# One step of a hybrid streaming encoder layer: weight split ahead of operands in the output projection, chunk states in groups of two, cached gate sum behind them

## Chip, cores and metric

The kernel runs on one core of one Trainium2 chip. The metric is the device time of one execution in microseconds (us), taken as the median of three runs. Engines are named as the profile names them: PE is TensorE's matmul stream and PEld its weight loads, DVE is VectorE, ACT is ScalarE, POOL is GpSimd, SP is SyncE (which here only issues DMAs).

## The reference, cut to what matters

One layer over 16 learned meta tokens and 512 prompt frames, and over 32 frames of a running stream with a cache of 256 rows. All branch inputs and gates come from one input projection. The GLA branch (gated linear attention) carries a state from chunk to chunk; the FoX branch (softmax attention with forget gates) needs running sums of the gate logs, for the running stream over cache and new frames together.

```python
def _gla_chunks(q, k, v, log_a, s0):
    g = jnp.cumsum(log_a, axis=2)
    g_tot = g[:, :, -1]
    k_dec = k * jnp.exp(g_tot[:, :, None] - g)
    u = jnp.einsum('bnchk,bnchv->bnhkv', k_dec, v)
    def step(s, inp):
        a, uc = inp
        s = jnp.exp(a)[..., None] * s + uc
        return s, s
    s_last, s_all = lax.scan(step, s0, (jnp.moveaxis(g_tot, 1, 0), jnp.moveaxis(u, 1, 0)))
    ...
# running stream: gate sums over the cached rows and the new ones
c_all = jnp.cumsum(jnp.concatenate([cache_logf.astype(jnp.float32), logf], axis=-1), axis=-1)
...
def _merge_ffn(h, ya, yb, ga, gb, w_out, norm_ffn, w_up, w_down):
    m = jax.nn.sigmoid(ga) * ya + jax.nn.sigmoid(gb) * yb
    h = h + jnp.einsum('btd,de->bte', m, w_out)
    u = jnp.einsum('btd,df->btf', _rmsnorm(h, norm_ffn), w_up)
    return h + jnp.einsum('btf,fd->btd', jnp.square(jax.nn.relu(u)), w_down)
```

## The kernel before

**Numbers in two halves.** Almost every matrix product runs on numbers split into a high and a low half in the matmul's 32-bit format: `split_hi` (L121, ACT) copies a tile into the format, `split_lo` (L124, DVE) subtracts the copy from the tile. A product is then three matmuls (hi*hi, lo*hi, hi*lo) into one PSUM tile. Both helpers have one line each, so in the trace tiles tell instructions apart, not lines.

**Weight units.** The projections' weights are a list of units of 128 output columns. `use(key)` makes sure that the unit asked for and the one after it are prepared (`unit_prep`): SP loads the raw weights `wr` (three buffers), POOL scales those of the input projection by the norm's gain (L250), ACT makes `wh`, DVE makes `wl`; `wh` and `wl` have two buffers each. A product over a unit (`blocks_steps`) is 48 matmuls: 8 row blocks, three products, two spans of tokens (288 and 256 columns).

**The order of work.** Up to the output projection the instructions are put in order by the framework's scheduler, which follows the order of the code as a priority; generators (`gq_steps`, `token_major` and others) are advanced a few steps at a time (`go(steps, n)`, `drain(steps)`) so that matmuls of one job stand between those of another. From `tc.manual_schedule` (ahead of the feed-forward part) on, PE, ACT and DVE run exactly in code order. A wait holds up all that stands behind it on its engine.

**GLA chunk states (L654 to L674, called at L804 to L806).** For each of five token tiles t (two chunks each) `chunk_states(t)` issues 8 products `ps_u` of 64 x 128 (the profile counts 16 matmuls, since these are not split), into the PSUM tiles `psv` (one buffer) and `psa` (two buffers), and then, per chunk, two DVE instructions that make the chunk's state from the one before (`states`, L671). Ahead of each tile 16 matmuls of the projection `ps_gq` (unit gq 0) are let through (`GAP_STATE`). After the five tiles the rest of gq 0 and all of gq 1 follow, then the small transposition `ps_prm` (L392), `ps_oS`, and the projection `ps_fv`.

**Cached gate sum (L723 to L731).** Ahead of that, `lS` collects the cached gate logs (a DMA that POOL issues) and the new ones (a POOL copy), a DVE scan turns `lS` into `cS`, and POOL writes `cS` to DRAM (`cSd`), from where it is read in the attention part. `cP` and `cPd` are the same for the prompt.

**Output projection (L1294 to L1305).** Eight units `wo`, in the order 0, 4, 1, 5, 2, 6, 3, 7; n counts them in this order. For each: `use` (prepares unit n+1), some steps of `pair_prep(0)` (weights for the first feed-forward pair: after n = 1 the loads, at n = 2 sums on DVE, at n = 4 four splits, at n = 6 three), 48 matmuls `ps_wo`, two DVE additions that take them into `xres` (L1300), and `operands(d)`. The last makes the feed-forward's inputs out of the unit just ended: for the first unit of a pair (d < 4) two ACT scalings `ba`, `bb`, a DVE difference (L1254) and a split `hh`/`hl`; for the second one scaling `b`, two DVE sums (L1261, L1262), three splits with another sum (L1273) between. The feed-forward's first product, `ps_x`, needs `hh` and `hl` of all four first units.

Of the kernel before, what the change touches and what calls it, by code (L numbers as in the profile page):

```python
# [13 lines left out]
ALU = mybir.AluOpType  # L14

P = 128
D = 1024
KD = D // P
SEQ = 512
META = 16  # L20
SMP = 32
PAST = 256
H = 8
# [24 lines left out]
def tile_hybrid_step(  # L48
# [8 lines left out]
    TE, ACT, DVE, POOL, SP = nc.tensor, nc.scalar, nc.vector, nc.gpsimd, nc.sync  # L57
# [29 lines left out]
    def tmp(shape, name, dtype=F32):  # L87
        return blk(shape, dtype, name, "tmp")
# [117 lines left out]
    onerow = tmp([SEQ], "onerow")[0:H]  # L206
# [11 lines left out]
    def drain(steps):  # L218
        for _ in steps:
            pass  # L220

    def go(steps, n):
        for _ in range(n):
            next(steps, None)
# [34 lines left out]
    def use(key, ahead=1):  # L259
        idx = [u[0] for u in units].index(key)  # L260
        while nxt[0] < len(units) and nxt[0] <= idx + ahead:
            unit_prep(nxt[0])
            nxt[0] += 1
        return done.pop(key)
# [112 lines left out]
    WO_ORDER = (0, 4, 1, 5, 2, 6, 3, 7)  # L377
# [265 lines left out]
    def decays(t):  # L643
# [7 lines left out]
        kd = g1[t][:, 0:256]  # L651
        DVE.tensor_tensor(kd[:n], dec[:n], kd[:n], ALU.mult)

    def chunk_states(t):  # L654
        c0, n = TT[t]
        kd = g1[t][:, 0:256]
        puv = [f(f"ps_u{t}").rearrange("p (a v) -> p a v", v=P) for f in (psv, psa)]
        for c in range(2):
            r0, r1 = (((0, META), (32, 64)) if t == 0 else ((0, 64), (64, 128)))[c]
            for hh in range(GH):  # L660
                mm(puv[c][64 * (hh % 2): 64 * (hh % 2) + 64, hh // 2, :],
                   kd[r0:r1, 64 * hh: 64 * hh + 64], gv[t][r0:r1, P * hh: P * hh + P], True, True)
        for c in range(2):
            ch = 2 * t + c
            dst = sblk[ch // 6][:, ch % 6]
            if ch == 0:
                DVE.tensor_copy(dst, puv[0][:, 0:2, :])
            else:
                prev = st0 if ch == 1 else (states[0] if ch == 2 else states[ch - 1])
                for p in range(2):  # L670
                    DVE.scalar_tensor_tensor(dst[:, p, :], prev[:, p, :], eg[:, p, ch: ch + 1], puv[c][:, p, :],  # L671
                                             ALU.mult, ALU.add)
            states[ch] = dst
    for t in range(NTT):  # L674
        totals(t)
# [44 lines left out]
    cP = tmp([META + SEQ], "cP")[0:H]  # L720
    DVE.tensor_tensor_scan(cP[:, 0:META], onerow[:, 0:META], lfa[:, 0:META], 0.0, ALU.mult, ALU.add)
    DVE.tensor_tensor_scan(cP[:, META:], onerow, lfb, cP[:, META - 1: META], ALU.mult, ALU.add)
    lS = tmp([PAST + SMP], "lS")[0:H]  # L723
    POOL.dma_start(lS[:, 0:PAST], cache_logf[0, 0])
    POOL.tensor_copy(lS[:, PAST:], lfa[:, 32:64])
    cS = tmp([PAST + SMP], "cS")[0:H]
    DVE.tensor_tensor_scan(cS, onerow[:, 0: PAST + SMP], lS, 0.0, ALU.mult, ALU.add)
    cPd = tc.dram_tile([H, META + SEQ], F32, name="cPd")
    cSd = tc.dram_tile([H, PAST + SMP], F32, name="cSd")
    POOL.dma_start(cPd, cP)  # L730
    POOL.dma_start(cSd, cS)  # L731


    V = [None] * NTT
# [67 lines left out]
    go(gq[0], 1)  # L802
    fv_steps = fv_prepare()
    for t in range(NTT):  # L804
        go(gq[0], GAP_STATE)
        chunk_states(t)  # L806
    drain(gq[0])
    drain(gq[1])
    late_params()
    POOL.dma_start(o_sp[0, 0].rearrange("(p a) k v -> (a k) p v", a=2), states[9])  # L810
# [483 lines left out]
    for n, d in enumerate(WO_ORDER):  # L1294
        xr = xres[d]
        wh, wl = use(("wo", d))
        go(prep, {1: 1, 2: 2, 4: 4, 6: 3}.get(n, 0))

        def evac_o(ci, a, b, ps, xr=xr):
            DVE.tensor_tensor(xr[:, a:b], ps, xr[:, a:b], ALU.add)  # L1300

        blocks(f"wo{d}", range(KD), wh, wl, lambda k, a, b: mh[k][:, a:b], lambda k, a, b: ml[k][:, a:b],
               OC, evac_o, psany, both=n == 0)
        hs[d] = xr
        operands(d, n == KD - 1)  # L1305


    ffnL = ctx.enter_context(ExitStack())
# [346 lines left out]
```

## Time and profile before

| | before |
|---|---|
| three runs | 831.92, 834.13, 834.67 us |
| median | 834.13 us |
| the profiled execution | 829.3 us |
| its span, first to last instruction | 827.5 us |
| PE busy (share of the span) | 801.3 us (97%) |
| PEld busy | 770.3 us (93%) |
| DVE, ACT, POOL busy | 584.0 us (71%), 366.6 us (44%), 123.6 us (15%) |
| mean granted TensorE clock | 0.997 |

The profile is of one execution; its times are microseconds from the first instruction. A row of the timeline gives the start, the length, the engine, the line, the operation with output and inputs, the shape, the number of instructions that it merges, and in brackets how long the engine stood idle before it and what ended that. The ends of matmuls are modelled, so the start of the next row is the better mark of how long a stretch took. The chain of waits follows the work that ended last back through what released each step.

### The profile page before, as it was taken

What the parts mean: (1) busy time and instruction counts of PE and PEld (TensorE: products, weight loads), DVE (VectorE), ACT (ScalarE), POOL (GpSimd) and SP (SyncE); (2) the same over time, 40 slices, a digit from 0 to 9 for tenths busy, and PEclk for the clock granted to TensorE, in tenths of its full rate; (3) what the DMA queues carried; (4) which work ended last, traced back from release to release, by engine and by line L of the source; (5) the groups of instructions that cost most, each with busy time, mean ns of one, the idle gap of its engine ahead of it and who ended that gap; (6) DMA issues with size and microseconds to landing.
All of it is one profiled execution on the core that took longest, in us unless ns stands there. A gap on an engine that the chain in (4) does not pass through costs nothing.

```text
span 827.5 us, 15155 instructions
## 1 busy us (share of the span) xinstructions
PE 801.3 (97%) x6093; PEld 770.3 (93%) x6093; DVE 584.0 (71%) x1142; ACT 366.6 (44%) x722; POOL 123.6 (15%) x132
## 2 busy tenths in 40 slices
PE   8998999999999999999989999999999999999995
PEld 7877899898999989999989999999999999999995
DVE  5856348798768464466567987778777776799764
ACT  6760454555345532323355783343334433433433
POOL 4305112221121384014100000000000000000000
PEclk9999999999999999999999999999999999999998
DMA  8513214431531123233522143323333332331402
GB/s 248 154 46 104 51 44 103 124 78 51 128 90 51 50 74 108 77 90 91 152 66 58 47 121 108 89 78 90 103 102 97 96 103 78 89 102 34 145 15 109
DMA packets 133813, 75.38 MB, mean 91 GB/s; under 512 B 15056, under 2 KB 129024, under 8 KB 133744
## 3 DMA queue, kind: packets, MB, share of 16 engines
q1 hardware_dynamic: 132560, 71.74, 30.9%
q0 software_dynamic: 1024, 2.14, 1.2%
q8 instruction: 48, 0.79, 0.4%
q10 hardware_dynamic: 160, 0.53, 0.2%
q14 instruction: 21, 0.17, 0.1%
HBM read 69.57 MB, written 4.83 MB: 90 GB/s over the span
## 4 chain that ended last, share of the span: by engine, by line
PE 73%; DVE 12%; ACT 5%; POOL 3%; issue 3%; DMA 3%; SPq 0%; ACTq 0%; POOLq 0%; DVEq 0%
PE ps_dn L118 23%; PE ps_x L118 11%; PE ps_v L118 6%; PE ps_gb L118 5%; PE ps_ga L118 5%; PE ps_fv L118 3%; PE ps_y L118 3%; PE ps_yb L118 3%; PE ps_ya L118 3%; PE ps_fk L118 2%; DVE wl L124 2%; PE ps_wo L118 1%; ACT wh L121 1%; DMA wr<-in_w_in_dram 1%; PE ps_s L118 1%
## 5 line engine op out<-in xcount | busy, mean ns | idle before, releaser
L118 PE MATMUL ps_dn<-uh,dl 128*128 128x288 f32 (+1 forms) x416 | 120.4, 289 | 0.0
L118 PE MATMUL ps_dn<-ul,dh 128*128 128x288 f32 (+1 forms) x416 | 119.8, 288 | 0.0
L118 PE MATMUL ps_dn<-uh,dh 128*128 128x288 f32 (+1 forms) x416 | 119.5, 287 | 0.0
L121 ACT ACTIVATE wh<-wr 128x1024 fp32r<-128x1024 f32 x46 | 48.5, 1055 | 87.9 <-PE ps_yb L118 24.4
L124 DVE TENSOR_TENSOR wl<-wr,wh 128x1024 fp32r<-128x1024 f32 x46 | 69.3, 1507 | 19.1 <-ACT wh L121 18.8
L250 POOL TENSOR_TENSOR wr<-wr,gmix 128x1024 f32<-128x1024 f32 x30 | 58.2, 1944 | 142.0 <-DMA wr<-in_w_in_dram 89.5
L118 PEld LDWEIGHTS ps_dn<-uh,dl 128*128 128x128 f32 x416 | 78.2, 188 | 0.2 <-DVE dl L124 0.2
L118 PEld LDWEIGHTS ps_dn<-uh,dh 128*128 128x128 f32 x416 | 78.4, 188 | 0.0
L118 PEld LDWEIGHTS ps_dn<-ul,dh 128*128 128x128 f32 x416 | 78.2, 188 | 0.0
L1504 DVE TENSOR_TENSOR acc<-ps_dn,acc 128x288 f32<-128x288 f32 x96 | 41.0, 437 | 30.1 <-PE ps_dn L118 30.1
L1329 POOL DMA_DIRECT2D gfin<-in_norm_final_dram x1 | 0.6, 607 | 369.6 <-DVE s3l L124 369.6
L124 DVE TENSOR_TENSOR dl<-dr,dh 128x512 fp32r<-128x512 f32 (+1 forms) x56 | 36.2, 647 | 1.6 <-ACT dh L121 1.4
L118 PE MATMUL ps_v<-hh,whi 128*128 128x272 f32 x120 | 34.8, 290 | 0.8 <-ACT fb L1416 0.6
L118 PE MATMUL ps_x<-hh,whi 128*128 128x272 f32 x120 | 35.0, 292 | 0.6 <-ACT fa L1407 0.6
L118 PE MATMUL ps_v<-hl,whi 128*128 128x272 f32 x120 | 34.7, 290 | 0.0
L118 PE MATMUL ps_x<-hh,wlo 128*128 128x272 f32 x120 | 34.6, 288 | 0.0
L118 PE MATMUL ps_x<-hl,whi 128*128 128x272 f32 x120 | 34.6, 288 | 0.0
L118 PE MATMUL ps_v<-hh,wlo 128*128 128x272 f32 x120 | 34.6, 288 | 0.0
L943 ACT ACTIVATE sb<-sb,m 128x144 f32<-128x144 f32 (+3 forms) x32 | 18.3, 573 | 35.2 <-DVE m L938 35.2
L124 DVE TENSOR_TENSOR wlo<-s,whi 128x512 fp32r<-128x512 f32 (+1 forms) x30 | 28.7, 956 | 6.7 <-ACT whi L121 6.7
L121 ACT ACTIVATE dh<-dr 128x512 fp32r<-128x512 f32 (+1 forms) x56 | 33.2, 593 | 0.0
L1434 ACT ACTIVATE x<-ps_x 128x272 f32<-128x272 f32 x16 | 6.3, 396 | 49.7 <-PE ps_x L118 49.6
(534 smaller groups left out, 2465.2 us busy)
## 6 DMA issues: line engine op xcount, KB each, us to landing
wr<-in_w_in_dram SPq DMA_DIRECT2D x30, 512.0 KB, 3.9
wr<-in_w_up_dram SPq DMA_DIRECT2D x58, 256.0 KB, 3.4
dr<-in_w_down_dram SPq DMA_DIRECT2D x48, 256.0 KB, 3.1
wr<-in_w_out_dram SPq DMA_DIRECT2D x8, 512.0 KB, 4.0
dr<-in_w_down_dram SPq DMA_DIRECT2D x8, 384.0 KB, 4.4
cb<-cPd SPq DMA_DIRECT2D x8, 264.0 KB, 4.0
x_t<-in_x_prompt_dram SPq DMA_DIRECT2D x4, 512.0 KB, 5.5
gvraw<-in_w_in_dram SPq DMA_DIRECT2D x4, 512.0 KB, 8.5
```

Of the source, the lines that this page charges most:

```text
L118: return TE.matmul(out, lhsT, rhs, start=start, stop=stop, skip_group_check=True)
L121: ACT.activation(out, in_, AF.Copy)
L124: (eng or DVE).tensor_tensor(out, in_, hi.bitcast(F32), ALU.subtract)
L250: POOL.tensor_tensor(raw, raw, gmix.unsqueeze(2).to_broadcast([P, KD, P]), ALU.mult)
L943: exps.append(ACT.activation(sb, sb, AF.Exp, bias=m, scale=-1.0, accum_out=rs).ins)
L1329: POOL.dma_start(late["gfin"], norm_final.partition_broadcast(P))
L1434: ACT.activation(x3, xv, AF.Copy)
L1504: DVE.tensor_tensor(acc[d][:, a:b], ps[:, :w], acc[d][:, a:b], ALU.add)
```

## The change

Two places change. In the output projection the operands of the unit ended are no longer made right behind its matmuls but in the next turn of the loop, behind `use`, which issues the split of the unit after (ACT `wh`, DVE `wl`). The last unit's operands follow the loop. In the GLA part, the chunk states of tiles 1 and 3 are issued right behind those of tiles 0 and 2, with no `ps_gq` matmuls let through between; odd tiles use both buffers of the PSUM tile `pss`. The load of the cached gate logs, the copy, the scan `cS` and the write `cSd` stand behind the five tiles and the rest of gq 0, and the scan is made to follow the last state's instruction on DVE.

```diff
@@ chunk_states
+    last_state = [None]
+
     def chunk_states(t):
         c0, n = TT[t]
         kd = g1[t][:, 0:256]
-        puv = [f(f"ps_u{t}").rearrange("p (a v) -> p a v", v=P) for f in (psv, psa)]
+        puv = [f(f"ps_u{t}").rearrange("p (a v) -> p a v", v=P) for f in ((psv, psa), (pss, pss))[t % 2]]
...
                 for p in range(2):
-                    DVE.scalar_tensor_tensor(dst[:, p, :], prev[:, p, :], eg[:, p, ch: ch + 1], puv[c][:, p, :],
-                                             ALU.mult, ALU.add)
+                    last_state[0] = DVE.scalar_tensor_tensor(dst[:, p, :], prev[:, p, :], eg[:, p, ch: ch + 1],
+                                                             puv[c][:, p, :], ALU.mult, ALU.add).ins
@@ gate sums
-    lS = tmp([PAST + SMP], "lS")[0:H]
-    POOL.dma_start(lS[:, 0:PAST], cache_logf[0, 0])
-    POOL.tensor_copy(lS[:, PAST:], lfa[:, 32:64])
-    cS = tmp([PAST + SMP], "cS")[0:H]
-    DVE.tensor_tensor_scan(cS, onerow[:, 0: PAST + SMP], lS, 0.0, ALU.mult, ALU.add)
...
     POOL.dma_start(cPd, cP)
-    POOL.dma_start(cSd, cS)
@@ GLA states
     for t in range(NTT):
-        go(gq[0], GAP_STATE)
+        if t % 2 == 0:
+            go(gq[0], GAP_STATE)
         chunk_states(t)
     drain(gq[0])
+    lS = tmp([PAST + SMP], "lS")[0:H]
+    POOL.dma_start(lS[:, 0:PAST], cache_logf[0, 0])
+    POOL.tensor_copy(lS[:, PAST:], lfa[:, 32:64])
+    cS = tmp([PAST + SMP], "cS")[0:H]
+    scan = DVE.tensor_tensor_scan(cS, onerow[:, 0: PAST + SMP], lS, 0.0, ALU.mult, ALU.add)
+    after(scan.ins, last_state)
+    POOL.dma_start(cSd, cS)
     drain(gq[1])
@@ output projection
         wh, wl = use(("wo", d))
+        if n:
+            operands(WO_ORDER[n - 1])
         go(prep, {1: 1, 2: 2, 4: 4, 6: 3}.get(n, 0))
...
         hs[d] = xr
-        operands(d, n == KD - 1)
+    operands(d, True)
```

**The order on PE in the GLA part.** First before, from the last matmul of unit gq 0 on. `ps_gq_0` and `ps_gq_1` are the two token spans, and `ps_gq_0_1014` begins unit gq 1; `ps_u_961` and `962` are token tile 2, `976` and `975` tile 3, `990` and `989` tile 4:

```order
L118 MATMUL ps_gq_1_920<-xl,wh_827 128x256
L118 MATMUL ps_u_961<-gvt_489,g1t 64x128 x4
L118 MATMUL ps_u_962<-gvt_489,g1t 64x128 x4
L118 MATMUL ps_u_976<-gvt_490,g1t 64x128 x4
L118 MATMUL ps_gq_0_1014<-xh,wh_834 128x288 x2
L118 MATMUL ps_u_975<-gvt_490,g1t 64x128 x4
L118 MATMUL ps_gq_0_1014<-xh,wh_834 128x288
L118 MATMUL ps_u_990<-gvt_490,g1t 64x128 x4
L118 MATMUL ps_gq_0_1014<-xh,wh_834 128x288 x4
L118 MATMUL ps_gq_0_1014<-xh,wl_835 128x288 x5
L118 MATMUL ps_u_989<-gvt_490,g1t 64x128 x4
```

and now, from the place in gq 0 at which tile 1 stood before (`938`, `939` are tile 2, `952`, `953` tile 3, `983`, `984` tile 4):

```order
L118 MATMUL ps_gq_1_928<-xh,wl_822 128x256 x2
L118 MATMUL ps_u_938<-gvt_489,g1t 64x128 x4
L118 MATMUL ps_u_939<-gvt_489,g1t 64x128 x4
L118 MATMUL ps_u_952<-gvt_490,g1t 64x128 x4
L118 MATMUL ps_u_953<-gvt_490,g1t 64x128 x4
L118 MATMUL ps_gq_1_928<-xh,wl_822 128x256 x5
L118 MATMUL ps_gq_1_928<-xl,wh_821 128x256 x7
L118 MATMUL ps_gq_1_928<-xh,wh_821 128x256
L118 MATMUL ps_gq_1_928<-xh,wl_822 128x256
L118 MATMUL ps_gq_1_928<-xl,wh_821 128x256
L118 MATMUL ps_u_983<-gvt_490,g1t 64x128 x4
L118 MATMUL ps_u_984<-gvt_490,g1t 64x128 x4
```

The five tiles now lie at three places inside gq 0 (tiles 0 and 1, 2 and 3, and 4 alone), and gq 1 follows unbroken; before, tiles 2 to 4 stood behind gq 0, and tiles 3 and 4 were taken apart between matmuls of gq 1.

**The order on DVE in the GLA part.** Before, behind the first two chunks' states (`qsS`, `qbdA`, `qbdB` take the projection gq out of PSUM):

```order
L789 SCALAR_TENSOR_TENSOR qsS<-ps_gq_0_838,rb 64x32
L789 SCALAR_TENSOR_TENSOR qbdA_820<-ps_gq_0_838,rb 64x4x64
L727 SCALAR_TENSOR_TENSOR cS<-onerow,lS 8x288
...
L671 SCALAR_TENSOR_TENSOR states_682<-states_682,eg,ps_u_930 128x128 x2
L671 SCALAR_TENSOR_TENSOR states_682<-states_682,eg,ps_u_931 128x128 x2
```

and now, behind the states of tile 3:

```order
L785 SCALAR_TENSOR_TENSOR qbdB_815<-ps_gq_1_928,rb 64x4x64 x2
L673 SCALAR_TENSOR_TENSOR states_683<-states_683,eg,ps_u_983 128x128 x2
L673 SCALAR_TENSOR_TENSOR states_683<-states_683,eg,ps_u_984 128x128 x2
L809 SCALAR_TENSOR_TENSOR cS<-onerow,lS 8x288
L124 TENSOR_TENSOR wl_1011<-wr_1007,wh_1010 128x1024
L785 SCALAR_TENSOR_TENSOR qsS<-ps_gq_0_1014,rb 64x32
```

The scan stood ahead of the states of tiles 1 to 4 and now stands behind all of them, ahead of a weight split (`wl_1011`, of the unit fk 0, used after `ps_fv`) and of gq 1's way out of PSUM. On POOL the load of `lS` and its copy changed places with the write of `cP`, and the write of `cS` went behind the write of the last state.

**The order on DVE in the output projection.** Before, from the way out of unit n = 3 on:

```order
L1300 TENSOR_TENSOR xres_4682<-ps_wo_1_4937,xres_4682 128x256
L1261 SCALAR_TENSOR_TENSOR bb_4899<-ba_4898,b_4963 128x272
L1262 TENSOR_TENSOR bb_4899<-b_4963,bb_4899 128x272
L124 TENSOR_TENSOR hl_4673<-bb_4899,hh_4669 128x544
L124 TENSOR_TENSOR hl_4673<-b_4963,hh_4669 128x544
L1273 SCALAR_TENSOR_TENSOR ba_4898<-bb_4899,b_4963 128x272
L124 TENSOR_TENSOR hl_4673<-ba_4898,hh_4669 128x272
L124 TENSOR_TENSOR wl_4977<-wr_4974,wh_4976 128x1024
L124 TENSOR_TENSOR a11l_4981<-u_4767,a11h_4980 128x512
```

and now:

```order
L1306 TENSOR_TENSOR xres_4682<-ps_wo_1_4937,xres_4682 128x256
L124 TENSOR_TENSOR wl_4966<-wr_4963,wh_4965 128x1024
L1265 SCALAR_TENSOR_TENSOR bb_4905<-ba_4904,b_4969 128x272
L1266 TENSOR_TENSOR bb_4905<-b_4969,bb_4905 128x272
L124 TENSOR_TENSOR hl_4673<-bb_4905,hh_4669 128x544
L124 TENSOR_TENSOR hl_4673<-b_4969,hh_4669 128x544
L1277 SCALAR_TENSOR_TENSOR ba_4904<-bb_4905,b_4969 128x272
L124 TENSOR_TENSOR hl_4673<-ba_4904,hh_4669 128x272
L124 TENSOR_TENSOR a11l_4981<-u_4767,a11h_4980 128x512
```

The split `wl` of the unit after next went from behind the six operand instructions to ahead of them; on ACT `wh` moved in the same way ahead of `b` and its three copies. The splits of `pair_prep(0)` stay behind both.

## Rows read from the trace of the kernel before

**Rows 1.** Page, part 1: busy us, share of span, instructions, by engine

```profile
PE 801.3 (97%) x6093; PEld 770.3 (93%) x6093; DVE 584.0 (71%) x1142; ACT 366.6 (44%) x722; POOL 123.6 (15%) x132
```

**Rows 2.** Windows: stretch, its length, PE busy (instructions), granted clock, DMA share, GB/s

```profile
62.37:82.17 19.80, 17.70 (x180) 1.00 0.39 103
398.07:404.13 6.06, 6.06 (x51) 1.00 1.09 284
404.13:445.98 41.85, 38.69 (x291) 1.00 0.27 77
```

**Rows 3.** Timeline of PE, GLA part (columns as told above)

```profile
64.81 0.68 PE L118 MATMUL ps_u<-gvt,g1t 16*64 16x128 f32 x16
65.42 0.81 PE L118 MATMUL ps_gq<-xl,wh 128*128 128x288 f32 x4
...
72.09 1.17 PE L118 MATMUL ps_u<-gvt,g1t 64*64 64x128 f32 x24 [1.80 <-DVE states L671]
...
74.02 0.65 PE L118 MATMUL ps_u<-gvt,g1t 64*64 64x128 f32 x8 [0.30 <-DVE states L671]
...
82.17 0.22 PE L392 MATMUL ps_prm<-ident,prm 9*128 9x9 f32 x1
```

**Rows 4.** Timeline of DVE, GLA part

```profile
69.10 1.65 DVE L727 TENSOR_TENSOR_SCAN cS<-onerow,lS 8x288 f32<-8x288 f32 x1 [1.93 <-DMA lS<-in_cache_fox_logf_dram]
...
71.34 1.12 DVE L671 SCALAR_TENSOR_TENSOR states<-states,eg,ps_u 128x128 f32<-128x128 f32 x4
...
74.31 1.22 DVE L124 TENSOR_TENSOR wl<-wr,wh 128x1024 fp32r<-128x1024 f32 x1
```

**Rows 5.** Timeline of POOL, GLA part (DMA issues)

```profile
64.15 0.50 POOL L724 DMA_DIRECT2D lS<-in_cache_fox_logf_dram  x1
...
65.03 0.51 POOL L730 DMA_DIRECT2D cPd<-cP  x1 [0.18 <-issue]
```

**Rows 6.** Chain of waits, behind the GLA part: start, length, what

```profile
127.09 1.07 ACT wh L121
...
273.28 0.03 DVE ptl L1063
273.30 5.10 DMA wr<-in_w_in_dram
```

**Rows 7.** Waits of PE: line, waited for, us in total, times, longest us

```profile
PE ps_wo L118 <- ACT wh L121: 2.8, 4, 0.8
```

**Rows 8.** Timeline of PE, output projection and first product behind it

```profile
417.57 1.20 PE L118 MATMUL ps_wo<-mh,wh 128*128 128x288 f32 x7 [0.69 <-ACT wh L121]
418.83 1.20 PE L118 MATMUL ps_wo<-mh,wl 128*128 128x288 f32 x7
...
445.98 0.29 PE L118 MATMUL ps_x<-hh,a11h 128*128 128x272 f32 x1
...
447.35 0.29 PE L118 MATMUL ps_x<-hl,a11h 128*128 128x272 f32 x1
```

**Rows 9.** Timeline of DVE, output projection

```profile
420.29 0.45 DVE L1261 SCALAR_TENSOR_TENSOR bb<-ba,b 128x272 f32<-128x272 f32 x1 [0.82 <-ACT b L1260]
...
424.02 0.44 DVE L124 TENSOR_TENSOR hl<-ba,hh 128x272 fp32r<-128x272 f32 x1 [0.50 <-ACT hh L121]
424.96 1.23 DVE L124 TENSOR_TENSOR wl<-wr,wh 128x1024 fp32r<-128x1024 f32 x1 [0.50 <-ACT wh L121]
...
428.51 0.78 DVE L1300 TENSOR_TENSOR xres<-ps_wo,xres 128x288 f32<-128x288 f32 x2
429.97 0.44 DVE L1254 TENSOR_TENSOR ba<-ba,bb 128x272 f32<-128x272 f32 x1 [0.67 <-ACT bb L1253]
431.13 0.73 DVE L124 TENSOR_TENSOR hl<-ba,hh 128x544 fp32r<-128x544 f32 x1 [0.72 <-ACT hh L121]
...
445.06 0.72 DVE L124 TENSOR_TENSOR hl<-ba,hh 128x544 fp32r<-128x544 f32 x1 [0.72 <-ACT hh L121]
```

**Rows 10.** Timeline of ACT, output projection

```profile
423.89 1.04 ACT L121 ACTIVATE wh<-wr 128x1024 fp32r<-128x1024 f32 x1
```

## The prediction

> **What bounds the kernel now.** I read the page first, then the chain of waits, the waits of PE, and the timelines of the two stretches that the diff touches. PE is busy for 97% of the span [rows 1], and the chain runs along PE nearly everywhere. So only time that PE loses in the two stretches can be won there, and what is won has to survive up to the end.
>
> In the GLA part PE needs 19.80 us from its first matmul of gq 0 (62.37) to `ps_prm` (82.17) [rows 2, 3]. It stands for 1.80 us ahead of tile 2's products and for 0.30 us ahead of a later half tile, each time for DVE's `states` [rows 3]. DVE is late because its scan `cS`, which none of this needs, stands ahead of the states of tiles 1 to 4: it waits 1.93 us for the load of `lS`, then takes 1.65 us [rows 4]. POOL issues that load at 64.15 [rows 5], so it took 4.95 us.
>
> In the output projection unit n = 1 runs its 48 matmuls without a gap in 6.06 us; the six units behind it take 41.85 us, 6.98 us each [rows 2]. The waits name the cause, ACT's `wh` [rows 7]: unit 4 starts 0.69 us late on `wh`, and its seven `wh` matmuls are followed only 1.26 us later by the `wl` ones, when DVE's `wl` is done [rows 8]. ACT and DVE make these splits last, behind the operands of an older unit: for unit 5 the operands fill DVE from 420.29 to 424.46, and only then come `wh` at 423.89 and `wl` at 424.96 [rows 9, 10].
>
> **The output projection.** Nothing is added or removed; `wh` and `wl` move ahead of the operands. `wh` of unit n+1 needs its raw weights and the buffer that unit n-1 leaves, so it can begin when unit n-1 ends: 1.04 us on ACT [rows 10], then 1.23 us on DVE [rows 9] behind two additions of 0.78 us together. Both are done some 2.5 us into unit n where DVE is not behind, and unit n+1 wants them 6 us in. Then every unit takes 6.06 us, and six of them 36.4 us in place of 41.85: **5.5 us** less. The bounds: 2.8 us, if only the waits that the profile names go [rows 7] and the slow first matmuls behind them stay, and 5.5. I take 5.5, since the unit at 398.07 has the same matmuls and ran without any of it.
>
> What is late next? The operands, now behind `wl`. By hand, for a pair of units on DVE: additions 0.78, `wl` 1.23, the long operands 4.17 (420.29 to 424.46), four splits of `pair_prep` 2.3 (`wl` and four splits take 3.55 from 424.96 to 428.51), additions 0.78, `wl` 1.23, the short operands 1.89 (429.97 to 431.86; their ACT part ahead of it now runs beside `wl`) [rows 9]. That is 12.4 us, against 12.12 us of matmuls: DVE is behind by up to half a unit inside a pair, but gains almost all of it back. The three pairs cost some 37.2 us, less one `wl` (unit 7 prepares none) and one split (three at n = 6), 35.4 to 35.7 us. From the end of unit 1 (404.13, plus 0.3 to the first addition) this gives the last `hl` at about 440.1, while PE ends unit 7 at 404.13 + 36.36 = 440.5 and wants that `hl` with the twelfth matmul of `ps_x`, 1.37 us later (445.98 to 447.35) [rows 8]. Before, it came at 445.78, 0.2 us ahead of the end [rows 8, 9]. So there is cover of 1.5 to 2 us, and the last unit's operands, as before, follow its additions. SP's queue keeps its order, and its loads wait for `wl`, so they go out earlier.
>
> Here the change adds a wait: DVE's `wl` waits for `wh`, which waits for PE; queued behind it are operands, splits and the next additions, and ACT's copies of the operands wait for those. The trace shows such queueing: the additions at 428.51 stand behind `wl` and four splits, though their unit, begun at 417.57, was long done [rows 8, 9]. The Trainium skill (TensorE: Matmul & The Clock Gate, Part 1, on engine queue depths) says that ScalarE and VectorE are strictly first in, first out. By that rule, on which the trace agrees, nothing slips past the wait, and a DVE that is the slower of the two would hold PE: that is the second rival below.
>
> **The GLA part.** The matmuls stay: two units of 6.06 us (same shapes as `ps_wo`), 12.12 us [rows 2], and five tiles of 16 products, 0.61 us each by the start of the next row (64.81 to 65.42) [rows 3], 3.05 us. Half tiles alone cost nearly as much, 0.65 us for 8 [rows 3]; they are whole again. With 0.1 us for each of some five changes between the two kinds, 15.7 us in place of 19.80: **4.1 us** less. The bounds are 2.1 us (the two named waits alone, 1.80 and 0.30) and 4.6 (no cost for changes); I take 4.1, since the parted tiles and the waits both go.
>
> Does a new wait take their place? With these durations tiles 0 and 1 end at 66.2 and tiles 2 and 3 begin at 68.2, after 16 matmuls of gq 0; DVE has tile 1's states by 67.6 (0.28 us each at 1.12 for four [rows 4]), so PSUM is free. Tile 4 begins at 71.4 and gq 1 runs from 72.1 to 78.2. DVE: tiles 2 and 3 until 71.2, gq 0's second span 0.85, tile 4 until 73.5, scan 1.65 until 75.2, `wl` 1.22 until 76.4, gq 1's first span some 1.1 until 77.5. `ps_oS` wants the last at about 78.2, so the scan's 1.65 us and the split are covered with 0.7 us to spare. The load of `lS` is moved behind the write of `cP` on POOL (65.03, 0.51 us [rows 5]), so it goes out at 65.5 and lands by 70.5, 3 us ahead of its scan. The write of `cS` goes out some 4 us later, behind the last state's; its readers belong to the attention part and come far later.
>
> **What carries on.** Behind `ps_prm` the chain is PE alone until ACT's `wh` at 127.09, then ACT, DVE and PE by turns. Its DMA pieces follow an instruction's end (273.28, then 273.30), so they move with it [rows 6]. I see nothing tied to a fixed time, and count 4.1 us in full. The clock is granted in full in both stretches [rows 2].
>
> **The sum.** 5.5 + 4.1 = 9.6 us. The profiled execution took 829.3 us, its span 827.5 and 1.8 us around it: 829.3 - 9.6 = 819.7. The median of the three runs is 834.13, 4.8 us above that execution; I take the gain off the median: **824.5 us**. By itself this case reaches from 823.8 to 826.0 (gains of 10.3 to 8.1), and with the spread of the runs (2.2 us down, 0.5 up) from 821.6 to 826.5.
>
> **Rivals.** First: the GLA gain is eaten in the attention part, where ACT and DVE take turns on the chain and a transfer could be the true pace [rows 6]. Against it, each transfer there is issued by what moves. Price 4.1 us: 828.6.
>
> Second, the queue rule at its worst: DVE and ACT become the bound in the output projection. If their chain of 35.7 us is 10% longer, the last `hl` comes at 443.7 and PE loses 1.8 us by `ps_x`; at 20% it comes at 447.3 and PE loses 5.4 us, all that was won there. Price 1.8 to 5.4 us: 826.3 to 829.9. For it speaks that 12.4 is above 12.12; against it that the durations are those of the same work, and the cover of 1.5 to 2 us.
>
> Third, slower than before: the load of `lS` lands late and the scan waits at its new place, with `wl`, gq 1's way out and `ps_oS` behind it. Every us past 74.2 costs one. It eats the GLA gain at 78.3 and all 9.6 us at 83.8, 18.3 us after its issue; a landing at 87 gives 837. Against it: 4.95 us in the trace.
>
> Fourth, the order isn't the one written, as where the scheduler parted tiles 3 and 4 before. The rows of the new order exclude it.
>
> **How the numbers follow.** The forecast 0.80, the first rival 0.08, the second 0.08, the third 0.02, and 0.02 that neither stretch gains. The range, 821.0 to 828.7, takes in the run spread and the bounds down to the first two rivals. About 0.3%, 2.5 us, is what a measurement here can tell from no change: faster means below 831.6. The first three cases are faster, though a loss in two of them at once ends near no change: faster 0.92, same 0.05, slower 0.03.
>
> **What would show it.** In the new profile: `ps_prm` near 78.1; no wait of PE for `states`, `cS` with little idle time ahead; no `ps_wo` wait for `wh` or `wl`; from unit 2 to `ps_x` 36.4 us; no wait in `ps_x` for `hl`. Wrong is the forecast if PE waits at `ps_oS` or `ps_x`, or if `wh` at 127 doesn't come 4 us sooner.

## The result and the profile of the changed kernel

The changed kernel took **821.78 us** (median of four runs, 821.63 to 822.02); the kernel before 833.02 us in the four runs beside it. The ratio is 0.9857, with a 95% interval of 0.9827 to 0.9888: faster, clear of the noise, by 1.4%. The forecast of 824.5 us was 2.7 us too high; the range held the time.

The page of the changed kernel, part 1 (as [rows 1]), and two windows of it: the GLA stretch from the first `ps_gq` matmul to `ps_prm`, and the six output units behind unit 1 (as [rows 2]; length, busy time and count of PE, PEld, DVE, ACT, POOL, then granted clock, DMA share, GB/s):

```profile
PE 796.5 (97%) x6093; PEld 768.5 (94%) x6093; DVE 585.9 (71%) x1142; ACT 367.2 (45%) x722; POOL 123.5 (15%) x132
...
63.77:79.56 15.79, 15.79 (x179) 14.54 (x177) 11.92 (x34) 1.35 (x2) 10.35 (x12) 1.00 0.49 127
402.03:438.35 36.32, 36.32 (x290) 36.32 (x289) 28.70 (x51) 20.69 (x33) 0.00 (x0) 1.00 0.32 89
```

PE is busy from end to end of both. 19.80 us became 15.79, 41.85 became 36.32: 4.01 and 5.53 us less, 9.54 together, where 4.1, 5.5 and 9.6 were forecast.

PE's timeline in the GLA part, which answers to [rows 3]; no row has an idle time in brackets any more:

```profile
66.20 1.29 PE L118 MATMUL ps_u<-gvt,g1t 16*64 16x128 f32 x32
...
69.62 1.15 PE L118 MATMUL ps_u<-gvt,g1t 64*64 64x128 f32 x32
...
72.69 0.68 PE L118 MATMUL ps_u<-gvt,g1t 64*64 64x128 f32 x16
...
79.56 0.22 PE L392 MATMUL ps_prm<-ident,prm 9*128 9x9 f32 x1
79.72 0.66 PE L118 MATMUL ps_oS<-qsS,states 128*128 128x64 f32 x4
```

DVE's, which answers to [rows 4]: the scan stands behind the last states, waits for nothing, and took 0.74 us where it took 1.65 before:

```profile
73.69 1.12 DVE L673 SCALAR_TENSOR_TENSOR states<-states,eg,ps_u 128x128 f32<-128x128 f32 x4
74.73 0.74 DVE L809 TENSOR_TENSOR_SCAN cS<-onerow,lS 8x288 f32<-8x288 f32 x1
75.40 1.19 DVE L124 TENSOR_TENSOR wl<-wr,wh 128x1024 fp32r<-128x1024 f32 x1
...
77.33 0.20 DVE L785 SCALAR_TENSOR_TENSOR qsS<-ps_gq,rb 64x32 f32<-64x32 f32 x1
```

In the output projection the waits of PE for `wh` [rows 7] are gone. What PE still waits for there (engine, line, releaser: us in total, times, longest) belongs to the first unit and to the feed-forward part:

```profile
PE ps_v L118 <- ACT fb L1422: 0.6, 1, 0.6
PE ps_x L118 <- ACT fa L1413: 0.6, 1, 0.6
PE ps_wo L118 <- ACT mh L121: 0.5, 1, 0.5
PE ps_wo L118 <- DVE ml L124: 0.2, 1, 0.2
```

So both terms of the sum came as worked out, and yet the two profiled executions differ by 7.5 us of span (827.5 and 820.0) and the medians by 11.2, neither by 9.6. The first gap is the stretch ahead of the change: in this execution of the changed kernel `ps_gq` began 1.40 us later (63.77 against 62.37), and 0.56 us was lost between `ps_prm` and the first output unit. That time is no effect of the change that any row shows: over all kernels here the first `ps_gq` matmul comes at 62.0 to 64.5 us, and the stretch from `ps_prm` to the first `ps_wo` takes 308.2 to 311.5 us. The second gap is what the experiments had to settle.

### The profile page after: what moved, and what is told of

Read it like the earlier page. It is cut to its first block, busy times and chain, and to the rows that moved or that the text cites. A ratio compares the mean times of both kernels' runs of the same rounds, so it can differ in the third digit from the quotient of the medians.

```text
span 820.0 us, 15157 instructions
## 1 busy us (share of the span) xinstructions
PE 796.5 (97%) x6093; PEld 768.5 (94%) x6093; DVE 585.9 (71%) x1142; ACT 367.2 (45%) x722; POOL 123.5 (15%) x132
## 3 DMA queue, kind: packets, MB, share of 16 engines
q0 software_dynamic: 1024, 2.14, 1.2%
## 4 chain that ended last, share of the span: by engine, by line
PE 79%; DVE 8%; POOL 4%; ACT 3%; DMA 3%; issue 2%; SPq 0%; ACTq 0%; POOLq 0%; DVEq 0%
PE ps_dn L118 23%; PE ps_x L118 11%; PE ps_v L118 6%; PE ps_gb L118 5%; PE ps_wo L118 5%; PE ps_ga L118 5%; PE ps_fv L118 3%; PE ps_y L118 3%; PE ps_yb L118 3%; PE ps_ya L118 3%; PE ps_fk L118 2%; PE ps_gq L118 2%; DMA wr<-in_w_in_dram 1%; PE ps_gv L118 1%; PE ps_s L118 1%
## 5 line engine op out<-in xcount | busy, mean ns | idle before, releaser
L124 DVE TENSOR_TENSOR wl<-wr,wh 128x1024 fp32r<-128x1024 f32 x46 | 72.1, 1566 | 17.9 <-ACT wh L121 17.6
```

Of the source, the lines that this page charges most:

```text
L124: (eng or DVE).tensor_tensor(out, in_, hi.bitcast(F32), ALU.subtract)
```

## Experiments

Each group of runs was taken on one chip beside the kernel before, whose median was 835.76 us (23 runs, 831.0 to 840.2) for the first four kernels, 835.80 (13 runs) for the next four and 835.53 (11 runs) for the last four. It is that spread that needs a cause: its profiled execution took 829.3 us. Two theories: the load of `lS`, on the path in the kernel before, **lands at varying times**; or the granted **clock falls** behind PE's stop in some executions.

The stretches of PE's timeline in each profiled execution, by the starts of rows (us): GLA part; `ps_prm` to the first `ps_wo`; units 0 and 1; units 2 to 7; from `ps_x` to the end.

| kernel | GLA | to `ps_wo` | units 0, 1 | units 2 to 7 | rest | span |
|---|---|---|---|---|---|---|
| before | 19.80 | 308.60 | 13.36 | 41.85 | 381.52 | 827.5 |
| before, again (b2) | 25.37 | 310.23 | 13.31 | 41.85 | 381.62 | 834.4 |
| output projection alone (e1) | 24.11 | 308.21 | 13.32 | 36.32 | 381.91 | 827.6 |
| GLA part alone (e2) | 15.79 | 309.23 | 13.33 | 41.84 | 381.62 | 826.3 |
| scan behind alone (e3) | 17.73 | 308.38 | 13.32 | 41.84 | 381.93 | 826.3 |
| groups of two alone (e4) | 18.45 | 310.37 | 13.31 | 41.86 | 381.97 | 828.5 |
| before, early load (e5) | 17.73 | 311.34 | 13.26 | 41.85 | 381.54 | 829.3 |
| changed, long stop (e6) | 27.41 | 310.96 | 13.29 | 36.32 | 381.72 | 832.0 |
| changed, short stop (e10) | 22.49 | 310.46 | 13.29 | 36.32 | 382.85 | 828.5 |
| changed, late load (e11) | 15.79 | 309.80 | 13.35 | 36.31 | 381.54 | 819.2 |
| changed, long operands (e9) | 15.80 | 311.54 | 13.25 | 37.43 | 383.95 | 826.0 |
| changed | 15.79 | 309.16 | 13.31 | 36.32 | 381.65 | 820.0 |
| changed, again (a2) | 15.79 | 308.83 | 13.33 | 36.32 | 381.85 | 818.3 |
| changed, `xres` behind (e8) | 15.79 | 310.04 | 12.01 | 36.32 | 381.93 | 818.7 |

### Output projection alone

```diff
@@ before, output projection
         wh, wl = use(("wo", d))
+        if n:
+            operands(WO_ORDER[n - 1])
...
-        operands(d, n == KD - 1)
+    operands(d, True)
```

> Only the output projection is changed (operands behind the next unit's split); the GLA part is as before. Theory (each of the two orders takes away its own stall, and nothing follows from one for the other): the six units behind unit 1 take 36.3 us in place of 41.85, the GLA stretch from its first ps_gq matmul to ps_prm stays at 19.8, and the time falls by 5.5 us. First rival (the gain is eaten behind): the stretch takes 36.3 but the rest grows, and the time falls by 4 us or less. Second rival (DVE and ACT become the bound): ps_x waits for hl, and the stretch to ps_x or ps_x itself takes 1.8 us or more longer. On the spread of the runs: if it is the load of lS that makes the runs of the kernel before differ by some 3 us, this kernel, which still waits for that load, spreads as much.

829.85 us (11 runs, 827.65 to 833.57), ratio 0.9946 (0.9924 to 0.9967), 5.9 us less. Units 2 to 7 take 36.32 us, as expected. The GLA part, which is word for word that of the kernel before, took 24.11 us and not 19.8. PE's timeline of this kernel shows the same stop of 1.8 us, and behind it the same matmuls taking longer: 8 of `ps_u` 1.12 us where they took 0.65 [rows 3]. Two rows of PE's timeline, then the windows, which show the clock:

```profile
73.46 1.17 PE L118 MATMUL ps_u<-gvt,g1t 64*64 64x128 f32 x24 [1.81 <-DVE states L671]
...
75.38 1.12 PE L118 MATMUL ps_u<-gvt,g1t 64*64 64x128 f32 x8 [0.29 <-DVE states L671]
...
63.73:73.46 9.73, 7.92 (x84) 7.11 (x81) 6.34 (x14) 1.34 (x2) 8.31 (x11) 1.00 0.54 140
73.46:75.38 1.92, 1.63 (x27) 1.21 (x27) 1.87 (x7) 0.00 (x0) 1.40 (x1) 0.91 0.02 5
75.38:84.56 9.18, 9.18 (x46) 7.66 (x47) 3.66 (x11) 0.00 (x0) 1.49 (x2) 0.50 0.25 66
84.56:87.84 3.28, 3.28 (x25) 3.15 (x25) 1.05 (x4) 0.00 (x0) 1.20 (x1) 0.89 0.07 21
```

Full clock up to the stop, then some ten us at 0.50, that is 1.2 GHz, the lower of TensorE's two levels. It costs 4.31 us (24.11 less 19.80). All eleven runs have a mean clock of 0.993 or less, which fits such a fall in each. The mean alone does not show it, for it doesn't tell where the clock fell: the changed kernel's profiled execution has a mean of 0.994 with the GLA part at full clock, and its lower level stands near the kernel's start:

```profile
7.75:14.58 6.83, 5.70 (x25) 5.62 (x25) 5.64 (x11) 4.94 (x12) 3.86 (x12) 0.50 1.06 296
```

One of that kernel's first four runs has 0.990 and took 821.71 us.

### GLA part alone

The changed kernel with `operands(d, n == KD - 1)` back at its old place at the end of the loop.

> Only the GLA part is changed (tiles in groups of two, scan and its load behind); the output projection is as before. Theory: the GLA stretch takes 15.8 us in place of 19.8, the six output units stay at 41.85, the time falls by 4.0 us. First rival (the gain is eaten in the attention part): the stretch is short but the output projection starts less than 3 us sooner. On the spread: if the load of lS is what varies, the runs of this kernel lie within 0.5 us of each other, and the fall against the kernel before can be larger than 4.0, up to 6 or 7 us.

826.91 us (6 runs, 825.69 to 828.32), ratio 0.9902 (0.9872 to 0.9931), 8.9 us less: more than the 4.0 us that the stretch shows (15.79), as the theory of a varying cost in that part has it; the trace itself is at full clock there. The runs spread over 2.6 us, more than the 0.5 expected. The gain is not eaten behind: `ps_prm` to the first `ps_wo` takes 309.23.

### Scan behind alone, and groups of two alone

```diff
@@ scan behind alone, against before: only the block of the cached gate sum moves
-    lS = tmp([PAST + SMP], "lS")[0:H]
...
-    POOL.dma_start(cSd, cS)
...
     drain(gq[0])
+    lS = tmp([PAST + SMP], "lS")[0:H]
...
+    POOL.dma_start(cSd, cS)
@@ groups of two alone, against before
-        puv = [f(f"ps_u{t}").rearrange("p (a v) -> p a v", v=P) for f in (psv, psa)]
+        puv = [f(f"ps_u{t}").rearrange("p (a v) -> p a v", v=P) for f in ((psv, psa), (pss, pss))[t % 2]]
...
-        go(gq[0], GAP_STATE)
+        if t % 2 == 0:
+            go(gq[0], GAP_STATE)
```

> Of the GLA part only the block of the cached gate sum (load, copy, scan, write) is moved behind the tiles; the tiles still come one by one, with 16 matmuls of gq between. Theory (the scan, with its wait for the load, is what makes DVE late with the states): PE's waits of 1.80 and 0.30 us for the states are gone, and the stretch takes 17.0 to 17.7 us, 2.1 to 2.8 less, so the time falls by 2.1 to 2.8. Rival (it is the two PSUM buffers, too few for five tiles, that hold PE): a wait of PE for states of 1 us or more stays, and the time falls by less than 1 us. On the spread: as for the kernel with the whole GLA change.

> Of the GLA part only the grouping is changed (tiles 0 and 1, 2 and 3 in one go, odd tiles in other PSUM buffers); the load of lS and its scan stay ahead. Theory (the scan is what makes DVE late): DVE still waits for the load ahead of the scan, now between the states of tile 1; a wait of PE for states of 1 to 2.5 us stays ahead of tile 2 or 3 and the stretch takes 17 to 19.5 us, the time falls by 0.3 to 2.8 us. Rival (the grouping with its four PSUM buffers is the whole gain): no wait of PE for states, the stretch takes 15.8, the time falls by 4.0 us. On the spread: if the load of lS is what varies, it spreads like the kernel before.

With the scan behind: 829.64 us (7 runs), ratio 0.9938 (0.9913 to 0.9963). The stretch is 17.73 us, 2.07 less, just the two waits (1.80 and 0.30), with one of 0.17 us left:

```profile
72.70 0.65 PE L118 MATMUL ps_u<-gvt,g1t 64*64 64x128 f32 x8 [0.17 <-DVE states L673]
```

With the groups alone: 831.13 us (12 runs), ratio 0.9948 (0.9927 to 0.997); the stop stays, and only the parted tiles are won back (18.45, 1.35 less). PE's timeline of that kernel:

```profile
68.39 1.09 PE L118 MATMUL ps_u<-gvt,g1t 64*64 64x128 f32 x24
71.56 0.65 PE L118 MATMUL ps_u<-gvt,g1t 64*64 64x128 f32 x8 [2.08 <-DVE states L671]
```

So the scan with its wait makes the stop, and PSUM buffers don't remove it. The two halves by themselves give 2.07 and 1.35 us, 3.42 in sum; both at once give 4.01, for only then are all tiles whole. The profiled execution of the groups alone had its 2.08 us stop and a full clock behind it; of its twelve runs the six with a mean clock of 0.996 or more took 828.4 to 831.0 us, the six with 0.992 or less 831.3 to 834.2.

### The kernel before once more

> The kernel before itself, for a profile of one more execution. In timed executions it mostly shows a granted clock of 0.991 and takes 834 to 837 us; the profile shown at the start had 0.997 and 829.3. Clock theory: if this execution has a clock of 0.992 or less, the clock is at half in a stretch of 8 to 11 us that begins within 3 us behind PE's stop ahead of tile 2, and the GLA stretch from the first ps_gq matmul to ps_prm takes 23.5 to 25 us in place of 19.80, with the same stop of 1.8 us. Landing-time rival: the load of lS lands later, the stop is 3 us or more longer, and the clock is full there.

One execution, 836.21 us, clock 0.987. Windows of the GLA part: up to the stop's end, tile 2, and the rest:

```profile
62.02:71.75 9.73, 7.92 (x83) 7.10 (x81) 6.22 (x14) 1.34 (x2) 8.32 (x11) 1.00 0.53 139
71.75:73.43 1.68, 1.68 (x25) 1.35 (x25) 1.63 (x6) 0.00 (x0) 1.42 (x1) 0.60 0.03 6
73.43:84.89 11.46, 11.46 (x58) 9.67 (x57) 5.05 (x16) 0.00 (x0) 2.69 (x2) 0.50 0.22 59
84.89:87.39 2.50, 2.50 (x18) 2.37 (x17) 0.00 (x0) 0.00 (x0) 0.00 (x0) 0.83 0.00 0
```

and the two engines at the stop:

```profile
68.97 1.43 DVE L727 TENSOR_TENSOR_SCAN cS<-onerow,lS 8x288 f32<-8x288 f32 x1 [2.14 <-DMA lS<-in_cache_fox_logf_dram]
...
71.75 1.74 PE L118 MATMUL ps_u<-gvt,g1t 64*64 64x128 f32 x24 [1.81 <-DVE states L671]
```

The same kernel as in [rows 2 to 4]: the load's wait is 2.14 us against 1.93 and PE's stop 1.81 against 1.80, but the stretch takes 25.37 us against 19.80. The 5.57 us lie wholly behind the stop, at half the clock. A second fall stands behind PE's wait of 1.50 us for `sb` in the attention part, which has 1.63 us more:

```profile
154.02:157.43 3.41, 3.41 (x18) 3.40 (x17) 3.13 (x6) 2.19 (x4) 0.00 (x0) 0.50 0.32 79
```

That is 836.21 against 829.3. So the landing time is not what differs between these two. The timed runs agree: of the 23, three with a mean clock of 0.996 or more took 831.00 to 831.84 us, fifteen with 0.991 or less 834.18 to 840.21, with a median of 835.97. (The rule is not strict: one run with 0.992 took 831.36. And even the three are 1.7 to 2.5 us above the profiled execution of 829.3, which the clock does not explain.)

### The stop taken away in the kernel before, and put back in the changed one

```diff
@@ early load, against before
     bfb = cq.tile([P, H], F32, name="bfb")
+    lS = cq.tile([P, PAST + SMP], F32, name="lS")[0:H]
+    POOL.dma_start(lS[:, 0:PAST], cache_logf[0, 0])
...
-    lS = tmp([PAST + SMP], "lS")[0:H]
-    POOL.dma_start(lS[:, 0:PAST], cache_logf[0, 0])
@@ long stop, against the changed kernel (PE is held to the written order besides)
+    held = [cPs.ins]
+    zero = DVE.memset(dead, 0.0)
...
+    for _ in range(6):
+        x = DVE.tensor_tensor(dead, dead, dead, ALU.add)
+        after(x.ins, held)
+        held = [x.ins]
@@ short stop: nine memsets in place of the additions
+    for _ in range(9):
+        x = DVE.memset(dead, 0.0)
```

`dead` is a buffer that nothing reads; the states of tile 0 are made to follow the last of these on DVE.

> The kernel before, with one thing changed: the load of lS is issued at the kernel's start, into a buffer of its own; the scan still stands ahead of the states on DVE, and the output projection is as before. Clock theory: the scan no longer waits 1.93 us, PE's stop ahead of tile 2 shrinks to 0 to 0.5 us, and with it the clock's fall goes; the GLA stretch takes 17.5 to 18.3 us, and the runs fall by 5 to 7 us against the kernel before, 2 from the stop and the rest from the clock. Landing-time rival: they fall by about 2 us against the quickest runs of before and lose the spread too. If the runs still spread over 5 us with a clock of 0.99 and less, the fall does not come from this stop.

> The changed kernel with a stop of PE put back by other means: six additions of 128 x 512 zeros on DVE (0.64 us each) ahead of the states of tile 0, and PE held to the written order, so that it stands about 2 to 3 us ahead of tile 2. No load is involved. Clock theory: the stop costs its 2 to 3 us in each run, and in most runs the granted clock falls to half behind it and costs 4 to 5 us more; the median rises by 5 to 8 us over the changed kernel, the runs spread over 3 us or more, and the low runs are those of a high clock. Landing-time rival: the median rises by 2 to 3 us alone, and the runs stay within 1 us.

> As the kernel with the stop put back, but with a shorter one: nine memsets on DVE (some 0.42 us each) ahead of the states of tile 0, and PE in exactly the order of the changed kernel. From the traces PE then stands about 1.3 us ahead of tile 2 and 0.8 us ahead of tile 3, as much as in the kernel before (1.80 and 0.30). No load is involved. Clock theory: the stop alone costs 1.5 to 2.5 us; in part of the runs, perhaps all, the clock falls behind it and costs some 4.3 us more: median 825 to 829.5, with a spread of 3 us or more, or all runs high and with a clock of 0.993 or less. Landing-time rival: 824 to 825 in all runs.

**Early load**: 829.72 us (6 runs, 828.35 to 831.17), ratio 0.9927 (0.9913 to 0.9941), 6.1 us less, though its GLA part saves only 2.07 (17.73): the scan stands where it stood, and with its input there in time it costs no more than behind the states. The other 4.0 us fit the clock, which is full there in the trace; the attention part of this execution (831.17, the slowest of the six) has a fall of its own, behind the same wait of 1.50 us as in b2:

```profile
63.58:81.31 17.73, 17.56 (x179) 15.46 (x176) 12.56 (x34) 1.35 (x2) 12.15 (x12) 1.00 0.44 114
147.17:150.58 3.41, 3.41 (x17) 3.39 (x16) 3.14 (x7) 2.81 (x5) 0.00 (x0) 0.50 0.30 65
```

**Long stop**: 833.46 us (7 runs, 832.53 to 835.01). One of the additions ran beside three of POOL's multiplications and took 6.30 us, not 0.64 (the others took 0.67 to 0.69), so PE stood for 6.06 us and not 2 to 3. **Short stop**: 830.03 us (6 runs, 829.39 to 832.11); its stop came out at 3.06 us, again longer than meant. The row of the stop and the window behind it, of the short stop:

```profile
72.66 2.79 PE L118 MATMUL ps_u<-gvt,g1t 64*64 64x128 f32 x24 [3.06 <-DVE states L674]
...
72.66:78.71 6.05, 6.01 (x40) 5.18 (x40) 3.59 (x14) 0.00 (x0) 0.79 (x1) 0.52 0.07 22
```

and the window behind the long one:

```profile
75.86:84.00 8.14, 8.14 (x43) 6.62 (x44) 4.26 (x16) 0.00 (x0) 0.79 (x1) 0.50 0.05 16
```

No load is involved in either, and the clock falls to half all the same. With the short stop the stretch grows by 6.70 us (15.79 to 22.49) for 3.06 us of standing: the other 3.6 us is the clock. All 13 runs of the two kernels have a mean clock of 0.995 or less (twelve of them 0.992 or less), and the runs of each lie within 2.7 us: that fits a fall in nearly every run, but for the timed runs it isn't shown.

Over all profiled executions: of the six with a stop of 1.8 us or more in the GLA part four have the lower level behind it (b2, e1, e6, e10), of the eight without such a stop none has it between 60 and 95 us. And the medians fall by more than the changed stretches do against the first trace of the kernel before: by 4.8 us more in e2, 4.1 in e3, 4.0 in e5 and 3.9 in the changed kernel (a2, below), where the stop is gone, but by 0.4 in e1, which keeps it, and by 3.3 in e4, which keeps it too but has a high mean clock in half of its runs. What stays open is a stop as short as that of the kernel before, 1.8 to 2.1 us: behind it the clock fell in two of the profiled executions (b2, e1) and not in two others (before, e4), and nothing in the traces tells why.

### The changed kernel again, and a late load

> The changed kernel itself, beside the others of this call. Theory (the kernel before loses, besides the stop of PE in the GLA part, some 4.3 us to a granted clock that falls to half behind that stop in most executions; the changed kernel has no stop there): the runs lie within 1 us of each other near 822, and the fall against the kernel before is 11 to 14 us, larger than the 9.5 us that the two traces without such a fall show. Rival (the load of lS lands at a time that varies from run to run): the same here; the next two kernels tell them apart.

822.36 us (5 runs, 820.36 to 824.89), ratio 0.9841 (0.9822 to 0.9859): 13.4 us less than the 835.80 beside it. The two changed stretches repeat to 0.01 us. The runs spread over 4.5 us, not the 1 us expected. The slowest (824.89) is the one with the lowest clock (0.992); falls in the attention part, which still has its stops, would do that, but the profile is of the quickest run and shows none there.

```diff
@@ late load, against the changed kernel
-    POOL.dma_start(lS[:, 0:PAST], cache_logf[0, 0])
+    POOL.dma_start(lD, cache_logf[0, 0])
...
+    POOL.dma_start(lE, lD)
+    POOL.dma_start(lS[:, 0:PAST], lE)
```

> The changed kernel with the load of lS made late: it goes through two DRAM buffers, each copy waiting for the one before on POOL's queue, so that it should land near 82 on the time line of the changed kernel, 7 us behind the end of the last state (74.8). The prediction's price for a late load (every us past 74.2 costs one): PE stops at ps_oS, and the GLA stretch grows by 7 to 7.5 us. The changed kernel's trace, where the scan took 0.74 us and DVE's work for ps_oS was done at 77.5, 2.2 us before PE wanted it: the stretch grows by some 5 us; the first 2.2 us are free. In both the clock may fall behind such a stop, which comes on top of the stop itself.

822.22 us (4 runs, 821.29 to 823.91), as the changed kernel. The last copy landed 2.5 us after its issue, so the load was only 2.3 us late, not 7. DVE and PE of this kernel:

```profile
75.79 0.75 DVE L814 TENSOR_TENSOR_SCAN cS<-onerow,lS 8x288 f32<-8x288 f32 x1 [2.34 <-DMA lS<-lE]
76.47 1.19 DVE L124 TENSOR_TENSOR wl<-wr,wh 128x1024 fp32r<-128x1024 f32 x1
77.58 0.17 DVE L785 SCALAR_TENSOR_TENSOR qsS<-ps_gq,rb 64x32 f32<-64x32 f32 x1
...
78.10 0.20 DVE L785 SCALAR_TENSOR_TENSOR qsS<-ps_gq,rb 64x32 f32<-64x32 f32 x1
...
78.35 0.66 PE L118 MATMUL ps_oS<-qsS,states 128*128 128x64 f32 x4
```

The scan waits 2.34 us, its followers on DVE come later by as much, the last `qsS` ends at 78.30, and `ps_oS` starts at 78.35 without a wait: the stretch stays at 15.79. The cover is used up to the last tenth. The slope beyond it was not tried.

### Longer operands

```diff
@@ against the changed kernel, in operands, behind the long operands of the first three pairs
+            for _ in range(4):
+                DVE.tensor_tensor(dead, dead, dead, ALU.add)
```

> The changed kernel with DVE's operand chain in the output projection made longer: four additions of 128 x 224 zeros (some 0.3 us each) behind the long operands of each of the first three pairs, 3.6 us in all, a tenth of the chain. Second rival's reckoning, by the changed kernel's trace: DVE's pair takes 12.1 us as PE's two units do, so nothing is made up; the last hl ends 3.6 us later, at 441.7, PE wants it at 439.7, and ps_x stands for 1.5 to 2.5 us; the units before it stay at 6.06 us. Rival: DVE has 7.6 us of idle time in these 36 us, which takes up the 3.6 us, and nothing is lost.

825.24 us (4 runs, 823.12 to 827.68), 2.9 us above the changed kernel's 822.36, which was measured in another group. The additions took 1.66 us a time, 5.0 in all. PE's timeline, where it now waits:

```profile
430.82 1.19 PE L118 MATMUL ps_wo<-mh,wl 128*128 128x288 f32 x7 [0.91 <-DVE wl L124]
...
442.05 0.29 PE L118 MATMUL ps_x<-hh,a11h 128*128 128x272 f32 x1
...
444.42 0.39 PE L118 MATMUL ps_x<-hh,a11h 128*128 128x272 f32 x1 [1.07 <-ACT hh L121]
...
445.18 0.39 PE L118 MATMUL ps_x<-hl,a11h 128*128 128x272 f32 x1 [0.24 <-DVE hl L124]
```

DVE does not make up for it, idle time or not. Units 2 to 7 grow by 1.11 us, for a `wl` queued behind the second addition block, and the rest by 2.3, of which the last operands' waits in `ps_x` are 1.3; where the other 1.0 us goes was not followed.

### A further step: the last `xres` behind the last sum

In the changed kernel PE still waits in the first output unit for `mh` and `ml` (0.5 and 0.2 us above), because on POOL four additions `xres` of 1.8 us stand ahead of the sum that `mh` is split from.

```diff
@@ against the changed kernel: POOL's last four xres behind the last sum of ga and gb
+        merged = POOL.tensor_tensor(sa, sa, sb_, ALU.add)
...
+        if len(xres) > 4:
+            after(xr.ins, [merged.ins])
```

> The changed kernel with one order on POOL turned: the four last additions xres stand behind the last addition of ga and gb, which feeds the last operands mh and ml of the output projection. In the changed kernel PE waits 0.52 us for that mh and 0.23 us for ml in the first output unit. Theory: both waits go and the first output unit takes 6.1 to 6.3 us in place of about 7.3; 0.7 to 1.0 us less than the changed kernel. Rival: the additions now run beside DVE's splits of the first output units and slow them, or the xres arrive late, and nothing is won or up to 1 us is lost.

820.79 us (5 runs, 819.64 to 822.44), ratio 0.9821 (0.9804 to 0.9837), against 0.9841 for the changed kernel in the same group. Units 0 and 1 take 12.01 us in place of 13.3. POOL's rows show the new order:

```profile
389.21 1.36 POOL L1207 TENSOR_TENSOR ga<-ga,gb 128x544 f32<-128x544 f32 x1 [4.60 <-DVE gb L1201]
390.53 7.77 POOL L1293 TENSOR_TENSOR xres<-xh,xl 128x544 f32<-128x544 f32 x4
```

The 1.3 us of units 0 and 1 is shown by the trace. That the kernel as a whole is faster than the changed one is not: the two groups of five runs overlap, and so do the intervals of their ratios.

## Why the prediction came out as it did

**The output projection** was right in size and reason: 5.5 us forecast, 5.53 measured, and 5.53 when done alone. Every unit takes 6.05 us. The upper bound was the right choice: with the queue cleared, the slow first matmuls behind each wait went too.

**Its cover** was right where it mattered. In the changed kernel the last `hl` ends at 438.15 and `ps_x`, begun at 438.35, wants it 1.37 us later: 1.57 us, inside the 1.5 to 2 worked out. A pair of units takes DVE 12.13 us (its additions stand at 411.14 and 423.27), not 12.4, so it keeps PE's pace and makes up nothing. That is why the second rival's price was nearly right: 5.0 us of added work, where the reckoning for a chain 10% (3.6 us) longer gave 1.8 and for 20% 5.4, cost 3.4 in the trace (the same reckoning for 5.0 gives 3.3). It left out that a `wl` further up runs out first.

**The GLA part** was right in size, 4.1 against 4.01, and its lower bound of 2.1 is what the scan alone gives (2.07). The durations behind it were not all right. I carried the scan's 1.65 us to its new place; it takes 0.74 there. At the old place it ran beside a POOL multiplication (below, on the hardware). The cover at `ps_oS` is not 0.7 us but 2.2, 0.9 of it more by the shorter scan: the last `qsS` ended at 77.53, and `ps_oS` began at 79.72. With it the third rival's price, "Every us past 74.2 costs one", was wrong: in the late load, whose `ps_gq` began at 62.41 as against 62.37, the scan began at 75.79, 1.6 us past 74.2, and cost nothing.

**What carries on** was right. `wh`, at 127.09 on the old chain [rows 6], comes at 124.44 in an execution whose `ps_gq` began 1.40 us later: measured from there, 4.05 us sooner. Of the first rival nothing is seen; `ps_prm` to the first `ps_wo` takes 308.2 to 310.4 us in the first four kernels with or without the GLA change.

**Two readings were loose.** The chain of waits runs along PE for 73% of the span by the page, not nearly everywhere; in the two stretches in question it made no difference. And the gains of 8.1 to 10.3 us, from which the range starts, do not follow from the bounds of the two terms, which add up to 4.9 to 10.1.

**The step that failed is the last of the sum**: "The median of the three runs is 834.13, 4.8 us above that execution; I take the gain off the median". That took the 4.8 us for a constant. The time came out 2.1 us above 819.7, the profiled execution less the 9.6, so of the 4.8 us 2.1 stayed (the quick runs of the kernel before, with a high clock, stand 1.7 to 2.5 above that execution too) and 2.7 went. Of these 1.1 is the base: with a fourth run its median is 833.02. The other 1.7 us, and in the second group 3.9 (13.4 less 9.5), is gain beyond the two stretches. The experiments put it down to the clock, which falls to half behind the very stop that the change removes; that fall cost 4.31 and 5.57 us in the traces of e1 and b2, and the profiled execution was one without it. For the four runs of the kernel before in the first group no clock is on record, so for them this is argued and not shown. The sentence that the clock "is granted in full in both stretches" was read off that one execution. So the base was wrong, and not the two terms. A profiled execution below every one of the timed runs should have been asked what the others had that it lacked.

## What to carry to other kernels

Work that nothing near needs, a scan or a split for later, belongs behind the work that the bottleneck waits for on each in-order queue; its price here was the wait for its input, not its own duration: with the load early and the scan left in place, the stretch was as short as with the scan moved. A stop of the bottleneck engine is worth more than its length if the clock falls behind it, so look at the granted clock of several executions before taking a gain off a median. Durations taken from a crowded place don't hold at a quiet one.

## What the runs showed of the hardware

**The clock behind a stop.** After a stop of 1.81 us TensorE ran at the lower level for most of the next 11 to 14 us in b2 and e1, at a cost of 5.57 and 4.31 us, and did not in two other executions with stops of 1.80 and 2.08 us. With stops of 3.06 and 6.06 us it fell in both profiled executions. Behind the wait of 1.49 to 1.53 us in the attention part, which all fourteen profiled executions have, it fell in two (b2 and e5).

**DVE beside POOL.** The scan took 1.65, 1.55, 1.43 and 1.31 us where it began 0.88, 0.98, 1.09 and 1.21 us after the start of a POOL multiplication of 1.91 us (before, e1, b2, e4). In all four it ended 0.61 to 0.62 us after that multiplication; with POOL's arithmetic idle it took 0.74. So it hardly moves until POOL is through. POOL's row in the kernel before, whose scan begins at 69.10 [rows 4]:

```profile
68.22 1.91 POOL L250 TENSOR_TENSOR wr<-wr,gmix 128x1024 f32<-128x1024 f32 x1
```

and in the long stop, where an addition that began just ahead of three multiplications took 6.30 us, ending 0.55 us behind the last of them, and a later one 0.69:

```profile
65.97 6.30 DVE L738 TENSOR_TENSOR dead<-dead 128x512 f32<-128x512 f32 x1
...
73.76 0.69 DVE L738 TENSOR_TENSOR dead<-dead 128x512 f32<-128x512 f32 x1
66.11 5.60 POOL L255 TENSOR_TENSOR wr<-wr,gmix 128x1024 f32<-128x1024 f32 x3
```

The `states` of the kernel before [rows 4], which read PSUM, kept 0.28 us each beside POOL. The Trainium skill (GPSIMD Engine Reference, 1. Specifications) says that the two engines share their SBUF interfaces, with contention for DVE instructions that read two SBUF inputs; these rows agree.

**The load of `lS`, three landing times.** It took 4.9 us from issue to landing in the kernel before, 3.9 in the changed one, 2.5 in e11, issued 6 to 9 us later and from a DRAM copy.
